# Modulation product of the second block's first layer: from TensorE to GpSimd in a two-block transformer kernel

## The chip, the core and the metric

The kernel runs on one core of a Trainium2 chip. The metric is the device time of one execution in microseconds (us). TensorE (PE) multiplies, VectorE (DVE) and ScalarE (ACT) work elementwise, GpSimd (POOL) works elementwise and issues transfers on a queue of its own, SyncE (SP) only issues transfers; all of them work through their instructions in the order in which the program lists them.

## What is computed

Two blocks in sequence over 256 tokens of 1024 features. The first block has two layers: an attention layer (dilated attention and gated linear attention) and a layer of gated scans. The second block has two layers as well, each a mixer with a feed-forward part, and both of its layers are modulated by a conditioning vector `c`. What matters here are three lines of the second block:

```
c_act = jax.nn.silu(c)
for l in range(DEPTH):
    mod = c_act @ w_ada[l] + b_ada[l]          # [1024] x [1024, 6144]
    sh_m, sc_m, g_m, sh_f, sc_f, g_f = [m[:, None, :] for m in jnp.split(mod, 6, -1)]
    h = rms_norm(x, norm_mix[l]) * (1.0 + sc_m) + sh_m
    ... # mixer; then g_m, sh_f, sc_f, g_f in the feed-forward part
```

`c` doesn't depend on the first block, so `mod` can be computed at any time before its use. For layer 0 of the second block the weights `w_ada[0]` are 6 chunks of 1024 columns, 24 MB in all. Chunks 0 and 1 are needed at the start of the mixer, chunks 2 to 5 behind it.

## The kernel before

**Linear layers.** Every large weight passes through `wtile` (line 210). It loads a block of up to 1 MB over SyncE's queue into a raw tile `wr` (line 220, two buffers), and splits it piece by piece (128 x 1024) into a high part `wh` (ScalarE, line 149) and a rest `wl` (VectorE, line 152). `lin_fm` and `lin_tm` run three matmuls for each pair of tiles: `xTh wh`, `xTh wl`, `xTl wh` (line 172). All matmuls of linear layers accumulate into tiles `pl`.

**The stages.** `layer_ab` runs from 0 to about 237 us: linear layers, two scan groups (class `Scan`, tiles `sc...`, partly on GpSimd), eight attention heads (`attn_a`, line 540), four heads of the linear attention, output layer. Each attention head loads a table `bt` (128 x 2 x 256, 256 KB) over GpSimd's queue (line 543). `layer_c` follows until about 518 us: three groups of linear layers, each with two scan groups on GpSimd, and on GpSimd also `1 - f` of the gates (line 514, tile `cf`). Both layers end with `out_ln` (line 594): its sums over feature tiles (`feat_sum`, tiles `lns`) are added on GpSimd (line 155) before TensorE sums them over the partitions; the layer norm that the next stage starts with waits for these sums. Then come the mixer of the second block's first layer (from about 518 us), its dense feed-forward part (from about 850 us), the second mixer, and the mixture of experts (from about 1406 us to the end).

**The modulation product before.** `ada` (line 699) makes one round of 1024 outputs: eight tiles `adaw` (128 x 1024, 512 KB, two buffers) over SyncE's queue (line 710), and for each of them four matmuls against the activated `c` (tile `adacs`), each in its own 32 rows of one bank `pl`. VectorE adds the bias tile `adao` (loaded by GpSimd, line 720, one buffer), and GpSimd writes the 1024 results to the scratch tensor `modd` (line 715), from which `prep_mod` (line 755, tile `modr`) reads them back as columns. The six rounds are called at: start of `layer_c` (line 458), its third group (line 508), start of the mixer (line 832), behind `solve` (two, line 868), behind the gates (line 886). For the second layer of the second block the product runs on VectorE (`ada_dve`, line 724, called from `wtile` by `self.hook`); that part isn't touched.

**The order.** The program is recorded in program order, and a scheduler orders the instructions of each engine from it before the run. On the chip each engine keeps that order: an instruction that waits holds up all that stand behind it on its engine.

Of the kernel before, what the change touches and what calls it, by code (L numbers as in the profile page):

```python
# [26 lines left out]
F32 = mybir.dt.float32  # L27
# [62 lines left out]
class Net:  # L90
    def __init__(self, ctx, tc, a, out, dump=None):
# [9 lines left out]
        self.hook = self.hold = None  # L101
# [5 lines left out]
        # the 8 banks: linear layers, and two kinds for everything else  # L107
# [34 lines left out]
    def warm(self, ps, cols, n=3, prev=None):  # L142
        """matmuls that keep the tensor engine's clock up while others decide"""
        for _ in range(n):
            i = self.mm(ps[:, :256], cols.to_broadcast([128, 128]), self.c["le1"][:, :256])
            self.behind(i, prev)
# [13 lines left out]
    def behind(self, ins, prev):  # L160
        """order of two instructions of one engine"""
# [16 lines left out]
    def trx(self, out, in_):  # L178
        """transpose into any partition quadrant"""
# [13 lines left out]
    def rsqrt(self, out, in_, scale, eps, pool):  # L193
        """out = (in * scale + eps) ** -0.5, with a step of Newton's method; in is overwritten"""
# [15 lines left out]
    def wtile(self, w, k0, nk, c0, ncol):  # L210
        """rows k0*128.. of w (nk tiles), columns c0..: list of (hi, lo) [128, ncol] per row tile"""
# [13 lines left out]
        for k in range(0, nk, step):  # L225
# [14 lines left out]
            if self.hold and self.hold[0]:  # L240
                self.hold[0] -= 1
                self.behind(ia, self.hold[1])
                self.behind(iv, self.hold[2])
            if self.hook:
# [6 lines left out]
    def mm3(self, out, A, B, start, stop):  # L251
        """out += A^T B with (hi, lo) operands"""
# [5 lines left out]
    def lin_fm(self, X, w, c0, ncols, KT, epi):  # L258
        """feature-major: epi(m0, ps [128, 2, 256]) for output rows m0*128.."""
# [12 lines left out]
    def lin_tm(self, X, w, c0, ncols, KT, epi, step=512):  # L272
        """token-major: epi(c, n, T, ps [128, n]) for output columns c.., token tile T"""
# [15 lines left out]
    def hilo(self):  # L289
        """operand of a layer's first or last product"""  # L290
# [4 lines left out]
    def pair(self, pool, use, dtype=F32):  # L295
        """work tile of two feature tiles; self.tags: where the layer has room for this use"""
# [6 lines left out]
    def feat_sum(self, pool, tag, on, out, first, last):  # L303
        """returns add(v): out [128, 256] = on^T summed over four pairs of feature tiles v [128, 2, 256]"""
# [17 lines left out]
    def load_x(self, pool):  # L322
        """the input, feature-major: residual and operand of the first layer"""
# [17 lines left out]
    def layer_ab(self):  # L341
        nc, tc, a = self.nc, self.tc, self.a
        with ExitStack() as cx:
# [8 lines left out]
            # Toeplitz table of bias and log multiplicity, times 8  # L352
# [14 lines left out]
            # gated linear attention  # L367
# [49 lines left out]
            # dilated attention  # L417
# [18 lines left out]
            # heads of the linear attention, each after its gate  # L436
# [14 lines left out]
    def layer_c(self):  # L451
        nc, tc, a = self.nc, self.tc, self.a
        with ExitStack() as cx:
# [4 lines left out]
            self.ada()  # L458
# [23 lines left out]
            for gr in range(3):  # L482
# [24 lines left out]
                if gr == 2:  # L507
                    self.ada()
# [21 lines left out]
    def load_cols(self, pool, src, n, tag, rtag=None):  # L530
        """rows [n, 128] of DRAM -> columns [128, n]"""
# [39 lines left out]
    def head_norm(self, p2, po, nv, gain, gate, yh, yl, ones, joint, eps=None, raw=None):  # L571
        """po [128, nv, 256]: rms over 128 rows (joint: over all nv*128), times gain, times gate -> hi, lo"""
# [21 lines left out]
    def out_ln(self, pool, Y, w):  # L594
        """z = alpha x + y w, in place of x, and the statistics of its layer norm"""
# [23 lines left out]
    def apply_ln(self, pool, layer, hi=None, lo=None, then=None):  # L619
        """x = layer_norm(z) from the statistics; hi, lo: its operand"""  # L620
# [20 lines left out]
    def square_sum(self, pool, pss, direct=False):  # L641
        """returns add(x): sums of squares over the features, four pairs of feature tiles"""
# [19 lines left out]
    def residual(self, pool, gate, direct=False):  # L662
        """returns epi(m, ps) of x += gate y and the function that ends it with the statistics of the rms norm"""
# [10 lines left out]
    def apply_rms(self, pool, sc, sh, hi, lo):  # L674
        """operand of x * rs * sc + sh"""
# [9 lines left out]
    def ada_init(self):  # L685
# [5 lines left out]
        self.ada_next, self.par, self.hook = 0, {}, None  # L691
# [5 lines left out]
        self.modd = [self.dp.tile([6, 4, 256], F32, name="modd%d" % l) for l in range(2)]  # L697

    def ada(self, n=1):
        """the next n of 6 rounds of silu(c) w_ada + b_ada of the first layer, 1024 values each, into scratch"""  # L700
# [118 lines left out]
    def mixer(self, l):  # L819
        nc, tc, a = self.nc, self.tc, self.a  # L820
        with ExitStack() as cx:
# [45 lines left out]
            if l == 0:  # L867
                self.ada(2)
# [891 lines left out]
```

## Time and profile before

| what | value |
|---|---|
| median of 3 runs | 2498.88 us (2495.86 to 2505.41) |
| span of the profiled execution, first to last instruction | 2500.5 us |
| TensorE, VectorE, ScalarE, GpSimd busy | 95%, 74%, 61%, 17% |
| mean granted TensorE clock | 0.981 of full speed |

The profiled execution has no time of its own beside its span: the span lies within the three runs, 1.6 us above their median. The profile lists instructions by engine and source line, names tiles as `out<-in`, and says for idle time what ended it. Matmuls are pipelined, so that two that follow each other overlap in the table; what one costs is read from the distance of two starts.

### The profile page before, as it was taken

The page shows a single profiled execution, that of the slowest core. Times are in us where ns is not written, and L with a number is a line of the kernel's source. Part 1 is how long each engine was busy: PE and PEld are TensorE (multiplying, and loading weights), DVE is VectorE, ACT ScalarE, POOL GpSimd, SP SyncE. Part 2 cuts the span into 40 slices and gives each one's busy share as a digit, 9 for nine tenths or more (in the row PEclk, how much of TensorE's full clock was granted, in tenths as well). Part 3 has the DMA queues.
Part 4 walks back from the last instruction along what each step waited for, and adds up shares of the span by engine and source line. Part 5 has one row for each costly group of instructions (what it writes and reads, how often), then busy time and mean ns, then how long its engine had stood idle before and what let it go on. Part 6 is the DMA issues. An engine that isn't in the chain of part 4 may idle for free.

```text
span 2500.5 us, 40457 instructions
## 1 busy us (share of the span) xinstructions
PE 2385.5 (95%) x15987; PEld 2016.8 (81%) x15987; DVE 1849.8 (74%) x2516; ACT 1517.0 (61%) x2164; POOL 426.3 (17%) x385
## 2 busy tenths in 40 slices
PE   7998999989999899999999989999999999999998
PEld 7877888868688799998788878787878787877776
DVE  5755777758754676676874578999888889888887
ACT  4654666547444443345754467787777676777765
POOL 2201320221100100001010122222222222222221
PEclk9999999999999899999999899999999999999999
DMA  6454446454443588875322659899999999999994
GB/s 196 150 129 153 154 136 208 144 190 144 123 141 114 174 270 275 279 246 153 102 74 64 236 220 369 317 353 340 368 337 344 330 351 335 339 337 349 329 347 170
DMA packets 335862, 586.90 MB, mean 235 GB/s; under 512 B 29984, under 2 KB 170528, under 8 KB 335664
## 3 DMA queue, kind: packets, MB, share of 16 engines
q1 hardware_dynamic: 321360, 577.28, 67.1%
q0 software_dynamic: 5504, 5.91, 1.3%
q8 instruction: 127, 2.08, 0.4%
q10 hardware_dynamic: 8800, 1.05, 0.3%
q14 instruction: 71, 0.58, 0.1%
HBM read 582.26 MB, written 1.64 MB: 234 GB/s over the span
## 4 chain that ended last, share of the span: by engine, by line
PE 68%; DVE 11%; issue 8%; DMA 5%; ACT 3%; POOL 1%; ACTq 0%; DVEq 0%; POOLq 0%
PE pl L172 43%; PE pn L172 16%; DVE wl L152 7%; PE pm L172 6%; ACT wh L149 2%; DMA wr<-in_w_dense_dram 2%; DMA adaw<-in_w_ada_dram 1%; PE pm L176 1%; PE pn L176 1%; DVE xf L158 1%; DMA wr<-in_w_in_c_dram 1%; DVE es L152 0%; POOL wl L155 0%; DVE ey L152 0%; DMA wr<-in_w_out_dram 0%
## 5 line engine op out<-in xcount | busy, mean ns | idle before, releaser
L152 DVE TENSOR_TENSOR wl<-wr,wh 128x1024 fp32r<-128x1024 f32 (+2 forms) x918 | 1193.0, 1331 | 347.4 <-ACT wh L149 338.1
L149 ACT ACTIVATE wh<-wr 128x1024 fp32r<-128x1024 f32 (+2 forms) x1004 | 1022.2, 1049 | 432.7 <-PE pl L172 229.6
L172 PE MATMUL pl<-wh,eg 128*128 128x512 f32 x1792 | 573.9, 395 | 0.0
L172 PE MATMUL pl<-xTh,wh 128*128 128x256 f32 x1696 | 485.9, 287 | 13.9 <-ACT wh L149 6.9
L172 PE MATMUL pl<-xTh,wl 128*128 128x256 f32 x1696 | 483.1, 286 | 0.3 <-DVE wl L152 0.2
L172 PE MATMUL pl<-xTl,wh 128*128 128x256 f32 x1696 | 482.7, 285 | 0.2 <-DVE xTl L158 0.2
L172 PEld LDWEIGHTS pl<-wh,eg 128*128 128x128 f32 x1792 | 336.8, 188 | 74.0 <-ACT wh L149 0.6
L172 PE MATMUL pl<-wl,eg 128*128 128x512 f32 x896 | 357.0, 398 | 15.8 <-DVE wl L152 11.8
L155 POOL TENSOR_TENSOR wl<-wr,wh 128x1024 fp32r<-128x1024 f32 x86 | 234.1, 2722 | 806.6 <-ACT wh L149 606.5
L172 PEld LDWEIGHTS pl<-xTh,wh 128*128 128x128 f32 x1696 | 324.0, 191 | 23.1 <-ACT wh L149 7.8
L172 PEld LDWEIGHTS pl<-xTl,wh 128*128 128x128 f32 x1696 | 323.7, 191 | 9.7 <-issue 7.7
L172 PEld LDWEIGHTS pl<-xTh,wl 128*128 128x128 f32 x1696 | 322.9, 191 | 9.1 <-issue 7.1
L172 PEld LDWEIGHTS pl<-wl,eg 128*128 128x128 f32 x896 | 168.4, 188 | 65.0 <-DVE wl L152 22.2
L172 PE MATMUL pn<-wl,eah 128*128 128x512 f32 x448 | 177.4, 396 | 4.3 <-DVE wl L152 4.3
L172 PE MATMUL pn<-wh,eal 128*128 128x512 f32 x448 | 174.7, 393 | 3.5 <-DVE eal L152 3.3
L172 PE MATMUL pn<-wh,eah 128*128 128x512 f32 x448 | 149.6, 394 | 3.5 <-ACT eah L149 3.5
L172 PEld LDWEIGHTS pn<-wl,eah 128*128 128x128 f32 x448 | 84.2, 188 | 24.4 <-DVE wl L152 6.6
L172 PEld LDWEIGHTS pn<-wh,eah 128*128 128x128 f32 x448 | 84.1, 188 | 23.7 <-ACT eah L149 5.0
L172 PEld LDWEIGHTS pn<-wh,eal 128*128 128x128 f32 x448 | 83.7, 188 | 21.9 <-DVE eal L152 4.8
L149 ACT ACTIVATE es<-pl 128x512 f32<-128x512 f32 x56 | 33.5, 599 | 93.3 <-PE pl L172 93.1
L172 PE MATMUL pl<-wl,xTh 128*128 128x440 f32 (+2 forms) x208 | 79.2, 381 | 9.1 <-DVE wl L152 9.1
L172 PE MATMUL pl<-wh,xTh 128*128 128x440 f32 (+2 forms) x208 | 74.3, 380 | 8.0 <-ACT xTh L149 5.7
(601 smaller groups left out, 3354.0 us busy)
## 6 DMA issues: line engine op xcount, KB each, us to landing
wr<-in_w_moe_dram SPq DMA_DIRECT2D x336, 1024.0 KB, 7.2
wr<-in_w_dense_dram SPq DMA_DIRECT2D x42, 1024.0 KB, 7.2
wr<-in_w_in_dram SPq DMA_DIRECT2D x32, 1024.0 KB, 5.2
wr<-in_w_in_c_dram SPq DMA_DIRECT2D x30, 1024.0 KB, 5.3
adaw<-in_w_ada_dram SPq DMA_DIRECT2D x48, 512.0 KB, 4.5
adar<-in_w_ada_dram SPq DMA_DIRECT2D x48, 512.0 KB, 5.6
wr<-in_w_in_ab_dram SPq DMA_DIRECT2D x16, 1024.0 KB, 5.3
wr<-in_w_in_dram SPq DMA_DIRECT2D x12, 880.0 KB, 4.7
```

The costliest lines, as they stand in the source:

```text
L149: return self.nc.scalar.activation(out, in_, f, **k)
L152: return self.nc.vector.tensor_tensor(out=out, in0=a, in1=b, op=op)
L155: return self.nc.gpsimd.tensor_tensor(out=out, in0=a, in1=b, op=op)
L158: return self.nc.vector.scalar_tensor_tensor(out=out, in0=a, scalar=s, in1=b, op0=op0, op1=op1)
L172: return self.nc.tensor.matmul(out=out, lhsT=l, rhs=r, start=start, stop=stop, **k)
L176: return self.nc.tensor.transpose(out, in_, self.ident[:k, :k])
```

## The change

`ada` and its six calls go. `ada_init`, in the first layer between the first linear layers and the scans, makes a generator `ada_pool`, and `wtile` takes one step of it for each piece of weights that it splits. 96 steps make the six rounds (8 row tiles, two halves of 512 columns each). A step loads 128 x 512 weights (256 KB) over GpSimd's queue into `adaw` (two buffers, half as wide as before), multiplies them by the column of `adacs` in place on GpSimd, and adds them on GpSimd to `adacc` (128 x 1024, one buffer). The last step of a round lets TensorE sum `adacc` over its partitions in four matmuls against ones, VectorE adds the bias, and GpSimd writes the result to `modd`. `mixer` runs whatever steps are left, before it does anything else. All else of the diff is comments and blank lines.

```diff
@@ wtile, behind the split of one piece
+            if self.hook0:
+                next(self.hook0, None)
@@ layer_c; the same at mixer, three places
-            self.ada()
@@ ada_init
-        self.ada_next, self.par, self.hook = 0, {}, None
+        self.par, self.hook = {}, None
...
+        self.hook0 = self.ada_pool()
@@ ada goes, ada_pool comes
-            ps = self.pl.tile([128, 512], F32, name="pl")
-            o = self.ada_bias(self.aw, 0, r)
-            for k in range(8):
-                raw = self.aw.tile([128, 1024], F32, name="adaw")
-                nc.sync.dma_start(out=raw, in_=w[k * 128:k * 128 + 128, r * 1024:(r + 1) * 1024])
-                for j in range(4):
-                    self.mm(ps[32 * j:32 * j + 32, :256], self.cs[:, k:k + 1].to_broadcast([128, 32]),
-                            raw[:, j * 256:(j + 1) * 256], k == 0, k == 7)
-            self.tt(o, o, ps[:, :256], OP.add)
-            nc.gpsimd.dma_start(out=self.modd[0][r], in_=o[0::32, :])
+        for r in range(6):
+            o = self.ada_bias(self.aw, 0, r)
+            acc = self.aw.tile([128, 1024], F32, name="adacc", bufs=1)
+            for k in range(8):
+                for hf in range(2):
+                    raw = self.aw.tile([128, 512], F32, name="adaw")
+                    c0 = r * 1024 + hf * 512
+                    nc.gpsimd.dma_start(out=raw, in_=w[k * 128:k * 128 + 128, c0:c0 + 512])
+                    v = acc[:, hf * 512:hf * 512 + 512]
+                    if k == 0:
+                        nc.gpsimd.tensor_scalar(v, raw, self.cs[:, 0:1], None, op0=OP.mult)
+                    else:
+                        nc.gpsimd.tensor_scalar(raw, raw, self.cs[:, k:k + 1], None, op0=OP.mult)
+                        nc.gpsimd.tensor_tensor(out=v, in0=v, in1=raw, op=OP.add)
+                    if k == 7 and hf == 1:
+                        ps = self.nbank()[:, :256]
+                        for j in range(4):
+                            self.mm(ps[32 * j:32 * j + 32], self.one.to_broadcast([128, 32]),
+                                    acc[:, j * 256:(j + 1) * 256])
+                        self.tt(o, o, ps, OP.add)
+                        nc.gpsimd.dma_start(out=self.modd[0][r], in_=o[0::32, :])
+                    yield
@@ mixer, first lines
+        for _ in self.hook0 or ():
+            pass
+        self.hook0 = None
```

The order moves at three places. **GpSimd behind the second scan of the first layer**: before, the table transfers `bt` of the heads and the sums `lns` of the output layer follow directly.

```order
L155 TENSOR_TENSOR scF<-scY,scR 128x96
L155 TENSOR_TENSOR scT<-scT,scR 128x32
L155 TENSOR_TENSOR scF<-scY,scT 128x96
L543 DMA bt<-tbd 128x2x256 x6
L155 TENSOR_TENSOR lns_2218<-xf 128x512
```

After, steps of the product stand there in pairs:

```order
L155 TENSOR_TENSOR scF<-scY,scT 128x96
L712 TENSOR_SCALAR adacc<-adaw,adacs 128x512 x2
L532 DMA cw0r<-in_conv_w_dram 48x128
L709 DMA adaw<-in_w_ada_dram 128x512 x2
L714 TENSOR_SCALAR adaw<-adaw,adacs 128x512 x2
L715 TENSOR_TENSOR adacc<-adacc,adaw 128x512 x2
```

The last three rows stand seven times before the next `bt`: two issues, two products that wait for their landing, two sums, and only then the next two issues.

**TensorE at the first head of the attention.** Before, the head (`pn<-ka,qa`) stands among matmuls of a linear layer:

```order
L172 MATMUL pl<-wh,xTh 128x512 x2
L172 MATMUL pn<-ka,qa 128x256 x2
L172 MATMUL pl<-wl,xTh 128x512
L172 MATMUL pl<-wh,xTl 128x512
L172 MATMUL pl<-wl,xTh 128x512
```

After, the sum over the partitions of round 0 (`pn<-adacc,kc`) stands in front of it, and the heads follow each other:

```order
L172 MATMUL pl<-xTh,wl 128x256
L172 MATMUL pn<-adacc,kc 32x256 x2
L172 MATMUL pn<-ka,qa 128x256 x2
L172 MATMUL pn<-bt,cst 128x256 x2
L172 MATMUL pn<-adacc,kc 32x256 x2
L176 MATMUL pm<-ident,as 128x128 x4
L172 MATMUL pn<-apt,va 64x256 x2
L172 MATMUL pn<-ka,qa 128x256 x2
```

Ahead of the first head stood 638 matmuls of linear layers (the scheduler's count, three for each pair of tiles); now there are 864.

**GpSimd at the end of `layer_c`.** Before, the sums `lns` of the output layer follow the last scan:

```order
L155 TENSOR_TENSOR scF<-scY,scR 128x96
L155 TENSOR_TENSOR scF<-scY,scT 128x96
L155 TENSOR_TENSOR lns_5532<-xf 128x512
L155 TENSOR_TENSOR lns_5534<-lnsq 128x512
L155 TENSOR_TENSOR lns_5532<-lns_5532,xf 128x512
```

After, the last pairs, the write of round 5 and the transfer `modr` that reads it back stand between the scan and these sums:

```order
L155 TENSOR_TENSOR scF<-scY,scT 128x96
L715 TENSOR_TENSOR adacc<-adacc,adaw 128x512
L709 DMA adaw<-in_w_ada_dram 128x512 x2
L714 TENSOR_SCALAR adaw<-adaw,adacs 128x512 x2
L715 TENSOR_TENSOR adacc<-adacc,adaw 128x512 x2
...
L722 DMA modd_616<-adao 4x256
L767 DMA modr<-modd_616 32x128
L155 TENSOR_TENSOR lns_5858<-xf 128x512
L155 TENSOR_TENSOR lns_5860<-lnsq 128x512
```

Four pairs stand in the place of the "...", the first of them shown. So all 96 steps stand between the second scan of the first layer and the sums that end the second layer. From the second half of the mixer on, the order of each engine is as before.

## Rows read from the trace of the kernel before

**Rows 1.** Page: span, and the chain of waits by engine.

```profile
span 2500.5 us, 40457 instructions
...
PE 68%; DVE 11%; issue 8%; DMA 5%; ACT 3%; POOL 1%; ACTq 0%; DVEq 0%; POOLq 0%
```

**Rows 2.** Windows: stretch, length, busy us of PE, PEld, DVE, ACT, POOL, clock, DMA share, GB/s.

```profile
97.60:237.00 139.40, 136.65 (x1025) 118.58 (x1026) 75.42 (x132) 67.96 (x119) 12.33 (x13) 1.00 0.46 129
237.00:509.50 272.50, 261.24 (x2469) 231.99 (x2468) 201.32 (x334) 168.09 (x249) 60.86 (x112) 0.97 0.51 166
509.50:538.00 28.50, 18.46 (x119) 12.23 (x117) 12.93 (x25) 10.84 (x20) 10.09 (x17) 0.82 0.66 214
600.00:716.00 116.00, 114.11 (x833) 84.01 (x831) 86.45 (x236) 65.15 (x152) 18.14 (x26) 1.00 0.45 138
```

**Rows 3.** All instructions on tile adaw, the modulation weights; durations in ns.

```profile
L172 PE MATMUL pl<-adaw,adacs x384: 377/379/636, 224.3 to 814.5; 128*32 128x256 f32 x192
L710 SPq DMA_DIRECT2D adaw<-in_w_ada_dram x48: 327/328/1077, 3.3 to 809.8; - x48
...
  DMA adaw<-in_w_ada_dram: 24.7, 13
...
DMA to landing us min/median/max: 3.6/4.5/14.8
```

**Rows 4.** Timeline of TensorE, start of the mixer: start us, us, instruction, idle before.

```profile
528.00 1.08 PE L172 MATMUL pl<-adaw,adacs 128*32 128x256 f32 x8 [3.78 <-DMA adaw<-in_w_ada_dram]
...
532.27 3.87 PE L172 MATMUL pn<-ln,kc 128*128 128x256 f32 x12
538.21 0.47 PE L172 MATMUL pl<-wh,xTh 128*128 128x440 f32 x1 [2.08 <-ACT xTh L149]
```

**Rows 5.** Timeline of TensorE inside the heads of the mixer.

```profile
694.03 0.64 PE L172 MATMUL pl<-adaw,adacs 128*32 128x256 f32 x8
694.59 0.39 PE L172 MATMUL pl<-xTh,wl 128*128 128x256 f32 x1
```

**Rows 6.** Chain of waits, 800 to 850 us: start us, us, what.

```profile
815.68 0.55 POOL modd L715
...
822.11 0.30 PE pm L176
```

**Rows 7.** Groups of GpSimd by line and shape: count | busy us, mean ns | idle before.

```profile
L155 POOL TENSOR_TENSOR mg<-mg,mg 128x512 f32<-128x512 f32 x6 | 9.3, 1544 | 19.4 <-DVE mg L152 19.4
...
L514 POOL TENSOR_SCALAR cf<-cf 128x1024 f32<-128x1024 f32 x6 | 8.5, 1423 | 94.4 <-ACT clf L149 94.4
...
L543 POOL DMA_DIRECT2D bt<-tbd x8 | 5.9, 737 | 76.7 <-PE pn L172 75.1 <-DMA tbd<-tb 1.6
...
L155 POOL TENSOR_TENSOR xf<-xTh,xTl 128x512 f32<-128x512 f32 x4 | 5.0, 1273 | 0.1
L155 POOL TENSOR_TENSOR lns<-xf 128x512 f32<-128x512 f32 x2 | 4.4, 2202 | 81.8 <-DVE xf L158 81.8
```

**Rows 8.** Tile bt, the 256 KB transfers of GpSimd: all eight, issue to landing.

```profile
DMA to landing us min/median/max: 4.7/4.8/8.3
```

**Rows 9.** Tile bt, 28 to 60 us: two such transfers issued together.

```profile
DMA to landing us min/median/max: 6.6/7.5/8.3
```

**Rows 10.** Timeline of GpSimd: end of the second scan, last sum of the second layer.

```profile
97.17 0.39 POOL L155 TENSOR_TENSOR scF<-scY,scT 128x96 f32<-128x96 f32 x1
...
508.26 1.29 POOL L155 TENSOR_TENSOR lns<-lns,lnsq 128x512 f32<-128x512 f32 x1
```

**Rows 11.** Waits of GpSimd: line, waited for: us in total, times, longest.

```profile
POOL adao L720 <- DMA modd<-adao: 34.4, 8, 7.0
```

**Rows 12.** Timeline of TensorE at the first head: spacing of the weight matmuls.

```profile
133.72 1.03 PE L172 MATMUL pn<-bt,cst 128*128 128x256 f32 x4
...
135.06 0.28 PE L172 MATMUL pl<-xTl,wh 128*128 128x256 f32 x1
135.18 0.28 PE L172 MATMUL pl<-xTh,wl 128*128 128x256 f32 x1
```

More of the change, by code (lines that the diff above doesn't have):

```diff
@@ L100, in __init__ @@
         self.wp = E(tc.tile_pool(name="wsplit", bufs=3))
-        self.hook = self.hold = None
+        self.hook = self.hold = self.hook0 = None
         self.wafter, self.moe_on, self.wfirst = None, False, []
@@ L506, in layer_c @@
                 self.lin_fm(X, w, 1536 + c0, 512, 8, epi_f(0))
-                if gr == 2:
-                    self.ada()
                 self.lin_fm(X, w, 3072 + c0, 512, 8, epi_f(1))
@@ L697, in ada_init, with ada_pool @@
         self.modd = [self.dp.tile([6, 4, 256], F32, name="modd%d" % l) for l in range(2)]
-    def ada(self, n=1):
-        nc = self.nc
-        for _ in range(n):
-            r = self.ada_next
-            self.ada_next += 1
-            w = self.a["w_ada_2"][0]
-            ps = self.pl.tile([128, 512], F32, name="pl")
+        self.hook0 = self.ada_pool()
+    def ada_pool(self):
+        nc, w = self.nc, self.a["w_ada_2"][0]
+        for r in range(6):
             o = self.ada_bias(self.aw, 0, r)
+            acc = self.aw.tile([128, 1024], F32, name="adacc", bufs=1)
             for k in range(8):
-                raw = self.aw.tile([128, 1024], F32, name="adaw")
-                nc.sync.dma_start(out=raw, in_=w[k * 128:k * 128 + 128, r * 1024:(r + 1) * 1024])
-                for j in range(4):
-                    self.mm(ps[32 * j:32 * j + 32, :256], self.cs[:, k:k + 1].to_broadcast([128, 32]),
-                            raw[:, j * 256:(j + 1) * 256], k == 0, k == 7)
-            self.tt(o, o, ps[:, :256], OP.add)
-            nc.gpsimd.dma_start(out=self.modd[0][r], in_=o[0::32, :])
+                for hf in range(2):
[16 more added lines that the diff above has]
+                    yield
     def ada_bias(self, pool, l, r):
@@ L831, in mixer @@
             if l == 0:
-                self.ada()
                 pss = self.nbank()[:, :256]
@@ L866, in mixer @@
             oa = solve()
-            if l == 0:
-                self.ada(2)
             mg = [p0.tile([128, 8, 256], F32, name="mg%d" % i, tag=("dq", "mg")[i]) for i in range(2)]
@@ L884, in mixer @@
             gate(0)
-            if l == 0:
-                self.ada()
             self.lin_fm(ob, a["w_ob_2"][l], 0, 1024, 4, branch_b)
```

## Prediction

> **What bounds the kernel now.** First the page: span 2500.5 us, and TensorE holds 68% of the chain of waits that ended last [rows 1]. Then the stretches that the change touches, from the end of the second scan of the first layer to the middle of the mixer [rows 2]: TensorE is busy 98% and 96% of the two long ones, GpSimd 12.33 of 139.4 us and 60.86 of 272.5 us. So up to 509.5 us TensorE is nearly the bound, and GpSimd has some 339 us to spare by its share. The question is whether the steps fit into them one behind the other. From 509.5 to 538 us TensorE is busy 18.46 of 28.5 us at a mean granted clock of 0.82, part of it at the lower of the two levels: the start of the mixer, with a round of the old product in it.
>
> **What goes.** The old product is 384 matmuls on TensorE (192, each in two passes), 48 issues on SyncE, and 24.7 us in which TensorE's two queues sat idle until `adaw` landed [rows 3]; some of it is one wait that both queues show. Eight of the 384 (one weight tile) cost 694.59 - 694.03 = 0.56 us of a full TensorE [rows 5]. Where it counts:
> - Start of the mixer. A group of the old product waits until 528.00 for its tile, and the sums of squares behind it (`pn<-ln`) come at 532.27 and hold up the first weight matmul until 538.21 [rows 4]. Without it these sums can follow ScalarE's squares: I take 6 us off.
> - Rounds 3 to 5 run among other matmuls in the mixer, where TensorE is busy 114 of 116 us [rows 2]: 24 groups x 0.56 = 13.4 us.
> - End of the mixer. The chain goes through the write of round 5 (815.68) and the read of `modr` to a transpose at 822.11 [rows 6]. After the change `modr` is read long before: 6 us off.
> Sum 25 us behind 509.5 us. The rounds before that (0 and 1, 16 groups x 0.56 = 9 us, and a few us of waits) count only if TensorE still bounds that stretch. On SyncE 48 issues of 0.33 us go, which weights no longer wait behind; I cost that at nothing, since after the change the weight transfers would share the engines with the same 24 MB from the other queue.
>
> **What comes.** 96 steps on GpSimd, in pairs, because `adaw` has two buffers and both are given back only by the sums. The order shows one pair: two issues, two products, two sums, then the next issues. Nothing is loaded ahead, so a pair is a round trip. Neither these transfers nor these operations are in the trace; the nearest rows:
> - Issue: 0.74 us (`bt`, also 256 KB) [rows 7]. The second one follows the first, and lands one issue later.
> - Landing: 4.8 us for `bt` alone, 4.7 at least [rows 8]; 6.6 to 8.3 us where two were in flight [rows 9]. The lower bound is 3.6 us, the least of a 512 KB tile of the same weights over SyncE's queue [rows 3]. I take 4.8, the same engine, queue and size.
> - Product, 128 x 512: half of the 1423 ns of 128 x 1024, 0.71 us [rows 7]. Only the second one lies behind the last landing.
> - Sum, 128 x 512: 1.27 us (`xf`) to 2.20 us (`lns`) [rows 7]; I take 1.5, near the 1544 ns of `mg`. Two of them.
> Round trip: 0.74 + 4.8 + 0.71 + 3.0 = 9.25 us, say 9.2. Ends: 0.74 + 3.6 + 0.6 + 2.54 = 7.5, and with a landing of 7.5 us 12.0.
>
> The Trainium skill gives another price (DMA: Bandwidth & Descriptors, section Anatomy of one DMA): a transfer issued from GpSimd takes about 2.0 us plus its bytes at 436 GB/s, that is an estimate of 2.6 us for 256 KB, and a round trip of 7.1 us. Rows 8 do not agree: 4.7 us is the least of eight.
>
> **Where it lies.** GpSimd works in order, and all 96 steps stand between the second scan, which ends at 97.56 us, and the sums `lns` that end `layer_c` (before: 509.55 us [rows 10]). The next stage can't start without those sums. So GpSimd's own time is a floor for that point:
> - start 97.6, products of the first pair (loaded ahead) 1.4;
> - 47 round trips x 9.2 = 432.4;
> - what GpSimd did there before, 12.33 + 60.86 = 73.2 [rows 2];
> - six times between rounds: the write to `modd` and the bias transfer, 1.3 us, and the wait of the second for the first, 34.4 / 8 = 4.3 us [rows 11]: 33.6;
> - minus what overlaps. Some scan pieces, `bt` issues and sums stand between an issue and the product that waits for it, and fill a wait that is there anyway. I take 30 off; the ends are 0 and 73.
> Sum 608 us, 99 us later than 509.55. The floor is also what holds the others up: TensorE's sum of round 0 stands ahead of the first head, so TensorE waits there from about 133.7 + 226 x 0.12 = 160.5 us (the 226 weight matmuls that now stand ahead, at the spacing of [rows 12]) until 97.6 + 1.4 + 7 x 9.2 = 163 us; then the scans of `layer_c`, whose pieces stand between pairs. Linear layers run ahead meanwhile, as far as their tiles allow, so that I add nothing for TensorE's own work behind 608. The half clock in the waits I cost at nothing too: TensorE has time left while it waits for GpSimd, and at the start of the mixer it already was at 0.82.
> Total: 2500.5 + 99 - 25 = 2574.5 us of span. The span is 1.6 us above the median, less than any term is known to: **2575 us**.
>
> **Rivals.**
> - Two in flight land later. If each pair waits as the two `bt` did [rows 9], the round trip is 12.0 us: 47 x 2.8 = 132 us more, 2706 us. For it: the weight blocks use half of the transfer engines in this stretch (share 0.46 and 0.51 [rows 2]). Against: the median of all eight `bt` is 4.8 [rows 8], and most were issued among weight blocks as well.
> - The round trip is short. At 7.5 us, the sum of the lower bounds, the floor falls by 80 us to 528, and the time is 2500.5 + 19 - 25 = 2494: no change that can be measured. It takes a landing below the least of `bt`, and sums beside an idle VectorE. By the rule of the Trainium skill's page (DMA: Bandwidth & Descriptors, section Anatomy of one DMA) it would be about 2475 us on the same working, which hangs on a landing that no row shows.
> - GpSimd isn't the bound: faster. This needs the chain to end before TensorE would, at about 509.55 - 13 = 496 us; from 97.6, with 78 us of other work after overlap, 47 round trips have 496 - 97.6 - 78 = 320 us, so it decides at 6.8 us, or where the order lets far more overlap than I took. Then all of the old product is gain: 25 + 13 = 38 us, 2462 us. But the heads of the attention lose their cover, since 226 weight matmuls moved ahead of them (27 us that used to fill their waits), so that half of the gain may go there. For it: GpSimd's idle share [rows 2]. Against: each round trip is mostly a wait, which idle time elsewhere doesn't shorten.
> - The steps do not stand where the diff puts them. The order rules this out: all 96 are there, and none is left for the mixer.
>
> **Chances.** Forecast (round trips of 8 to 10.5 us) 0.63, its own range 2520 to 2640. Slower landings or more stalls through TensorE and VectorE, which wait in order for each round, 0.16, around 2700. Short round trip 0.12, around 2494. GpSimd not the bound 0.09, 2462 to 2480. A measurement of this kernel tells about 0.5% from no change, 12.5 us. Faster by over that: 0.09 and a little of the short round trip, 0.11. Within: the rest of it, 0.10. Slower: 0.79. The range leaves out the last case and the upper half of the slow one: 2494 to 2680.
>
> **What would show it.** In the trace after: the distance of two pairs of `adaw` issues on GpSimd is the round trip, 9.2 us, most of it idle until `adaw` lands. The sums `lns` of `layer_c` end near 608 us. TensorE is idle in `layer_ab` and `layer_c` for some 100 us, with GpSimd or `adacc` as the releaser, and its clock falls there. The first weight matmul of the mixer comes 6 us sooner behind the last sum than before, and from there to the end it is 25 us shorter in all. The prediction is wrong if the round trip is below 7 us, if the pairs overlap in spite of two buffers, or if GpSimd sits idle for anything but its own transfers in between.

## The result, and the profile after

The changed kernel takes 2656.4 us (median of 4 runs, 2646.4 to 2672.8) against 2499.9 us: 1.064 times as long, 95% interval 1.060 to 1.068. The forecast was 2575 us, with 2680 as the upper end of the range: the way is right, the loss is twice as large as forecast (157 against 75 us). The profiled execution has a span of 2671.0 us, near the top of the runs.

The page shows first that this is no longer a kernel of TensorE alone. Busy time by engine, and the chain of waits by engine and by line (before: TensorE 68%, GpSimd 1% [rows 1]):

```profile
PE 2415.8 (90%) x15651; PEld 2042.0 (76%) x15651; DVE 1909.5 (71%) x2516; ACT 1519.8 (57%) x2164; POOL 774.9 (29%) x661
...
PE 62%; DVE 11%; POOL 11%; DMA 8%; issue 4%; ACT 4%; ACTq 0%; SPq 0%; DVEq 0%; POOLq 0%
```

The windows show where. Columns are start and end, length, busy us of PE, PEld, DVE, ACT and POOL, TensorE's granted clock, DMA share, GB/s. The stretch from the first product to the end of `layer_ab`, and `layer_c`:

```profile
102.00:307.00 205.00, 157.76 (x1054) 125.01 (x1053) 96.35 (x135) 68.28 (x120) 133.39 (x115) 0.83 0.43 128
307.00:695.00 388.00, 285.78 (x2427) 252.94 (x2428) 243.89 (x340) 171.01 (x251) 294.90 (x294) 0.85 0.43 140
```

Before, the two together took 412 us with TensorE busy over 95% at a clock of 1.00 and 0.97 [rows 2]; now they take 592 us, it is busy 75% of them, and the mean clock of 0.84 means that part ran at the lower of its two levels, behind its waits. So the loss lies ahead of one point, the sums `lns` that end `layer_c`: their end moved from 509.6 to 694.4 us (start and length of the last one, from the timeline of GpSimd). The forecast had 608.

```profile
693.10 1.28 POOL L155 TENSOR_TENSOR lns<-lns,lnsq 128x512 f32<-128x512 f32 x1
```

All instructions on `adaw` in the changed kernel, as in [rows 3]; durations in ns (minimum, median, maximum):

```profile
L709 POOL DMA_DIRECT2D adaw<-in_w_ada_dram x96: 536/574/647, 12.0 to 652.0; - x96
L714 POOL TENSOR_SCALAR adaw<-adaw,adacs x84: 1552/1567/3586, 111.0 to 656.2; 128x512 f32<-128x512 f32 x84
L715 POOL TENSOR_TENSOR adacc<-adacc,adaw x84: 1249/1290/2311, 115.5 to 658.9; 128x512 f32<-128x512 f32 x84
L712 POOL TENSOR_SCALAR adacc<-adaw,adacs x12: 1561/1904/3017, 102.0 to 583.4; 128x512 f32<-128x512 f32 x12
...
  DMA adaw<-in_w_ada_dram: 96.2, 41
  PE pn L172: 18.2, 1
...
DMA to landing us min/median/max: 3.0/3.7/7.2
```

The product takes 1.57 us where the forecast had 0.71; the landing 3.7 us (least 3.0) where it had 4.8. The timeline of GpSimd shows one undisturbed pair (start, duration, operation, count, and in brackets the idle time before it):

```profile
232.90 1.09 POOL L709 DMA_DIRECT2D adaw<-in_w_ada_dram  x2
236.01 3.27 POOL L714 TENSOR_SCALAR adaw<-adaw,adacs 128x512 f32<-128x512 f32 x2 [2.02 <-DMA adaw<-in_w_ada_dram]
239.26 2.47 POOL L715 TENSOR_TENSOR adacc<-adacc,adaw 128x512 f32<-128x512 f32 x2
241.68 1.13 POOL L709 DMA_DIRECT2D adaw<-in_w_ada_dram  x2
```

From issue to issue 8.8 us, of which only 2.0 are idle. Last, the longest waits of GpSimd from 102 us to the end of `layer_c`, and of TensorE up to 700 (engine, line, releaser: us in total, times, longest):

```profile
POOL adaw L714 <- DMA adaw<-in_w_ada_dram: 95.3, 40, 5.7
POOL adacc L712 <- PE pn L172: 18.2, 1, 18.2
POOL modr L767 <- PE pm L176: 17.3, 1, 17.3
POOL bt L542 <- PE pn L172: 12.9, 6, 4.3
...
POOL lns L155 <- DVE xf L158: 6.8, 1, 6.8
POOL modd L722 <- DVE adao L152: 6.5, 3, 3.9
POOL cf L513 <- ACT clf L149: 3.1, 1, 3.1
```

```profile
PE pn L172 <- POOL adacc L715: 77.8, 6, 29.5
```

TensorE waits 77.8 us for running sums that GpSimd has not finished; GpSimd waits 65 us for TensorE, VectorE and ScalarE (the rows below the first). Each of the two works in order, and each is held up by the other.

### The profile page after: what moved, and what is told of

Its sections match the earlier page's. It is cut to its first block, busy times and chain, and to the rows that moved or that the text cites. A ratio compares the mean times of both kernels' runs of the same rounds, so it can differ in the third digit from the quotient of the medians.

```text
span 2671.0 us, 40003 instructions
## 1 busy us (share of the span) xinstructions
PE 2415.8 (90%) x15651; PEld 2042.0 (76%) x15651; DVE 1909.5 (71%) x2516; ACT 1519.8 (57%) x2164; POOL 774.9 (29%) x661
## 4 chain that ended last, share of the span: by engine, by line
PE 62%; DVE 11%; POOL 11%; DMA 8%; issue 4%; ACT 4%; ACTq 0%; SPq 0%; DVEq 0%; POOLq 0%
PE pl L172 37%; PE pn L172 17%; DVE wl L152 7%; PE pm L172 6%; DMA adaw<-in_w_ada_dram 4%; POOL adaw L714 4%; POOL adacc L715 3%; ACT wh L149 2%; DMA wr<-in_w_dense_dram 2%; PE pm L176 1%; PE pn L176 1%; POOL adacc L712 1%; DVE xf L158 1%; POOL wl L155 0%; POOL scY L155 0%
## 5 line engine op out<-in xcount | busy, mean ns | idle before, releaser
L152 DVE TENSOR_TENSOR wl<-wr,wh 128x1024 fp32r<-128x1024 f32 (+2 forms) x918 | 1215.1, 1355 | 346.4 <-ACT wh L149 342.8
L714 POOL TENSOR_SCALAR adaw<-adaw,adacs 128x512 f32<-128x512 f32 x84 | 150.8, 1800 | 95.7 <-DMA adaw<-in_w_ada_dram 95.3
L715 POOL TENSOR_TENSOR adacc<-adacc,adaw 128x512 f32<-128x512 f32 x84 | 125.8, 1511 | 0.3
```

The costliest lines, as they stand in the source:

```text
L152: return self.nc.vector.tensor_tensor(out=out, in0=a, in1=b, op=op)
L714: nc.gpsimd.tensor_scalar(raw, raw, self.cs[:, k:k + 1], None, op0=OP.mult)
L715: nc.gpsimd.tensor_tensor(out=v, in0=v, in1=raw, op=OP.add)
```

## Experiments: how much of it is GpSimd, and by what

In all runs below, "end" is the end of the last `lns` of `layer_c` in the profiled execution, and VectorE's time is its busy time from the first product to that end. From this end to the end of the program it is 1963 to 1968 us in e1, e2, f1 and f2, 1977 in the changed kernel, 1957 to 1987 in all runs that leave none of the product to the mixer (e3 apart, see there), and 1991 before. So, to some 15 us, the end of `layer_c` is what the runs are compared by.

| kernel | time, us | ratio to before (95%) | end, us | VectorE, us |
|---|---|---|---|---|
| before | 2500 | 1 | 509.6 | 277 |
| changed | 2656.4 | 1.060 to 1.068 | 694.4 | 340 |
| e1, no product at all | 2473.3 | 0.988 to 0.994 | 501.7 | 278 |
| e2, arithmetic on 4 columns | 2507.7 | 1.001 to 1.007 | 532.9 | 279 |
| f2, product of two operations | 2578.3 | 1.029 to 1.038 | 605.5 | 348 |
| j1, e2 with fillings | 2572.7 | 1.024 to 1.031 | 598.7 | 297 |

**e1, the product left out**:

```
- nc.gpsimd.dma_start(out=raw, in_=w[k * 128:k * 128 + 128, c0:c0 + 512])
- nc.gpsimd.tensor_scalar(raw, raw, self.cs[:, k:k + 1], None, op0=OP.mult)
- nc.gpsimd.tensor_tensor(out=v, in0=v, in1=raw, op=OP.add)
+ if k == 0 and hf == 0:
+     nc.gpsimd.memset(acc, 0.0)
```

> The changed kernel without the 96 transfers, products and sums of the first layer's modulation (the running sum is set to zero once per round, so the modulation is its bias alone); the six sums over partitions on TensorE, the bias transfers and the writes stay. Left out is therefore all that GpSimd does for the product. Theory A (GpSimd's in-order chain of pairs sets when layer_c ends): the last lns falls from 695 to about 500, where TensorE's own work ends, and the time from 2656 to about 2462. Rival B (the order itself costs: heads without the weight matmuls that covered their waits, linear layers behind one another): the chain of GpSimd was only part of it, the heads still wait, lns ends at 530 to 560, time 2490 to 2520.

2473.3 us, end at 501.7, 11 us above theory A's time and at its end: the order of the heads costs nothing that matters, all 183 us of gain come with GpSimd's steps. It is also what this order would give if the product cost nothing, some 27 us less than before.

**e2, transfers without arithmetic.**

```
- nc.gpsimd.tensor_scalar(raw, raw, self.cs[:, k:k + 1], None, op0=OP.mult)
- nc.gpsimd.tensor_tensor(out=v, in0=v, in1=raw, op=OP.add)
+ nc.gpsimd.tensor_scalar(raw[:, :4], raw[:, :4], self.cs[:, k:k + 1], None, op0=OP.mult)
+ nc.gpsimd.tensor_tensor(out=v[:, :4], in0=v[:, :4], in1=raw[:, :4], op=OP.add)
```

> The changed kernel with all its transfers, but each product and each sum over 4 of the 512 columns only, except the first product of each half of a round, which stays whole (so most of the modulation's sum is left out). Landing waits and issues stay, arithmetic goes. Theory A by the measured pieces: a pair falls from 8.7 us (1.1 issues, 2.0 of landing left, 3.1 products, 2.5 sums) to 1.1 + 3.7 + 0.4 = 5.2 us; 48 pairs take 250 us instead of 420, the chain ends near 102 + 250 + 77 = 430, before TensorE is done, so the time falls to that of the kernel without any of it or some 20 us above: 2462 to 2490. Rival C (the landings and the queue are what costs): the pair stays above 7.5 us and the time above 2580.

2507.7 us, 18 above the expectation's upper end, with 85.4 us of waits for landings still there. Transfers, issues, landing waits and the small operations that are left cost 34 us, the arithmetic that was taken out 149. Theory C falls.

**e3, a constant as the scalar; f2, the product as two operations.** Why does a product of 512 columns take longer than the constant one of 1024 from which the forecast had taken its price [rows 7]? First the scalar, `self.cs[:, k:k + 1]` replaced by 0.5:

> The changed kernel with the constant 0.5 in place of the column of the activation as the scalar of each product on GpSimd (the modulation's values are wrong; nothing else differs). It asks why a product of 128x512 took 1.57 us where the constant one of 128x1024 took 1.42. If the per-partition scalar is the cause, the product falls to about 0.71 us; a pair then is 1.1 + 2.0 + 0.7 + 0.9 (product, or the rest of the second landing) + 2.5 = 7.2 us instead of 8.7, 48 x 1.5 = 72 us less on GpSimd's chain, 2580 to 2600 by theory A. If the price belongs to the type, the shape or the place, the product stays at 1.57 and the time at 2656.

The product took 1.49 us: it is not the scalar. (Behind `layer_c` this run is not comparable. It executes some 12,400 more instructions, presumably since other modulations send other tokens to the experts, and 3660 us says nothing of the change.) Then the form; the row of 1024 columns is an instruction of two operations:

```
- nc.gpsimd.tensor_scalar(raw, raw, self.cs[:, k:k + 1], None, op0=OP.mult)
+ nc.gpsimd.tensor_scalar(raw, raw, self.cs[:, k:k + 1], 0.0, op0=OP.mult, op1=OP.add)
```

> The changed kernel with the product written as two operations of one instruction (times the scalar, plus 0.0), as the instruction of 128x1024 that took 1.42 us has two; the values are the same. The run with a constant as the scalar left 1.49 us of the 1.57, so the per-partition scalar is not why the product is dear. If the form with a single operation is, the product falls to about 0.75 us, a pair to 7.2 us and the time by some 72 us to 2575 to 2600. If not, product and time stay as they are (1.57 us, 2656).

```profile
L714 POOL TENSOR_SCALAR adaw<-adaw,adacs x84: 682/700/5060, 105.5 to 558.3; 128x512 f32<-128x512 f32 x84
```

0.70 us instead of 1.57, and 2578.3 us instead of 2656.4: 78 us for adding zero. The forecast's price was right for the form of its row, and the kernel uses the other form.

**e4 and f1, loads ahead.** Written one step ahead (the load of step i + 1 ahead of the product of step i), the transfers should have hidden their landings:

> The changed kernel with each transfer issued one step ahead: the load of step i + 1 stands before the product of step i, in the same two buffers. Nothing is left out. Theory A: 3.4 us of issue, product and sum per step stay (0.57 + 1.57 + 1.25), the landing (3.7 us from its issue) has 2.8 us of arithmetic to hide behind and mostly does, so that the 96 us of waits for landings fall to 20 to 50; 45 to 75 us less, time 2580 to 2610. Rival C (the transfers' own durations bind, the queue serves them no sooner): waits stay near 96 and the time within 15 us of 2656. Rival D (it is not GpSimd's own time but the mutual waits with TensorE and ScalarE): GpSimd is sooner at its steps and waits for the others instead, time 2630 to 2656.

2648.8 us, a miss of theory A: the scheduler still put GpSimd's instructions in pairs (two loads, two products, two sums), and it waited 89.6 us for landings. Program order is not engine order here. With the order pinned:

```
+ nx = load() if todo else None
  i = nc.gpsimd.tensor_scalar(raw, raw, self.cs[:, k:k + 1], None, op0=OP.mult)
+ self.behind(i, nx)
```

> In the run with loads written one step ahead GpSimd's instructions still came in pairs (two loads, two products, two sums), so that it changed nothing and waited 89.6 us for landings. Here the order of one engine is pinned as well: the product of step i is put behind the issue of the load of step i + 1, nothing is left out. Theory A: a step is 0.57 + 1.57 + 1.25 = 3.4 us plus what is left of a landing of 3.2 to 3.7 us behind 2.8 us of arithmetic, 0.4 to 0.9 us: 3.8 to 4.3 instead of 4.4 to 5.4; waits for landings fall from 96 to 40 to 60 us, time 2600 to 2625. If the mutual waits with TensorE take what is saved, the time stays within 15 us of 2656.

2631.1 us, 6 above the expected interval. Waits for landings fell from 96 to 8.1 us and the end came 35 us sooner: the waits for TensorE rose instead (`adacc` 21.5, `bt` 18.6).

**f3 and f4, the steps spread into the mixer** (f4: with the pinned loads of f1):

```
- next(self.hook0, None)
+ self.h0 = getattr(self, "h0", 0) + 1
+ if self.h0 * 96 // 176 != (self.h0 - 1) * 96 // 176:
+     next(self.hook0, None)
```

> The changed kernel with its 96 steps spread evenly over 176 weight blocks, those of the mixer's first half included (rounds 2 to 5 are read only behind the mixer): 70 steps stand ahead of the sums that end layer_c instead of 96, and 26 in the mixer. Nothing is left out. Theory A: 26 steps x 4.4 us = 114 us less on GpSimd's chain ahead of these sums, lns ends near 580, and the mixer has room on GpSimd (26 of 284 us busy): time about 2540, up to 2565 where the steps stand in the way of the mixer's own GpSimd work. If what costs is the product's total on GpSimd wherever it stands, or the order of the heads, the time stays above 2620.

> Both: steps spread over 176 weight blocks and each load pinned ahead of the product of the step before it. Nothing is left out. Theory A: 70 steps x 3.8 to 4.3 us = 266 to 300 us ahead of the sums that end layer_c, with 102 of start and 77 of other work 445 to 480 us plus the mutual waits (65 us with 96 steps, in proportion 47): 492 to 527, just about where TensorE's own work ends (502 without the product). Time 2475 to 2510. If mutual waits don't shrink with the steps, 2530 to 2560.

f3 took 2551.4 us, inside its expectation, but by two errors against each other: the end came at 537.6 and not near 580, and the part behind it grew from 1977 to 2022 us. f4 missed: 2567.7 us, end at 546, not sooner than f3 in spite of the shorter steps. In the mixer GpSimd waited 77.1 us (f3) and 83.4 us (f4) in one piece for TensorE to read the running sum. Fewer us on GpSimd are not the same as a sooner end.

**g1 to g3, every step made cheap.** Half rounds (a running sum of 128x512), three buffers, loads pinned two steps ahead, product of two operations. g3 is g1 spread as f3; g2 is g1 with product and sum on VectorE:

```
- i = nc.gpsimd.tensor_scalar(raw, raw, self.cs[:, k:k + 1], 0.0, op0=OP.mult, op1=OP.add)
- nc.gpsimd.tensor_tensor(out=acc, in0=acc, in1=raw, op=OP.add)
+ i = self.stt(acc, raw, self.cs[:, k:k + 1], acc, OP.mult, OP.add)
```

> The changed kernel with the two-operation product (0.70 us instead of 1.57 in the run before), half rounds one after the other (a running sum of 128x512), which makes room for a third transfer buffer, and each load pinned two steps ahead. Nothing is left out. Theory A: a step is 0.58 issue + 0.70 product + 1.29 sum = 2.6 us, the landing (3.2 us) hides behind two steps; 96 x 2.6 = 247 us, with 100 of start and 77 of other GpSimd work 424, plus mutual waits of 50 to 65 us as far as these come at all: 474 to 490, so that TensorE's own work sets the end of layer_c, at 502 to 515; time 2473 to 2490. If the mutual waits grow into the room (each wait of GpSimd for TensorE is a wait of TensorE for GpSimd later), lns ends at 530 to 560 and the time is 2500 to 2530.

> The transfers stay on GpSimd's queue (three buffers, two steps ahead, half rounds), but the product and the running sum are one instruction of VectorE (1.28 us for 128x1024 in the second layer's modulation, so about 0.65 for 128x512: 84 x 0.65 + 12 x 0.4 = 60 us of VectorE), each pinned behind the rest of the weight block at which it is written. Nothing is left out. Theory A: GpSimd keeps 96 issues x 0.58 = 56 us and waits for buffers rather than landings; VectorE has room (some 330 of 505 us busy ahead of the end of layer_c); lns ends at 505 to 520, time 2475 to 2495. If VectorE's 60 us stand ahead of the rests that TensorE waits for, 2510 to 2540.

> As the run with half rounds, two-operation products and loads two steps ahead, but with the 96 steps spread over 176 weight blocks, into the mixer. Nothing is left out. Spreading had cost 57 us behind layer_c in the two runs that did so (26 steps among the mixer's own GpSimd work), at 4.4 us a step; with 2.6 us it is about 35. Theory A: ahead of layer_c's end GpSimd has 100 + 70 x 2.6 + 77 = 359 us of work, and TensorE sets it (502 to 510); time 2473 + 35 = 2500 to 2515, more than the run that is not spread. If the end of layer_c is still set by GpSimd with 96 steps, spreading gains instead: 2475 to 2490, less than that run.

All three missed theory A's times, and this is where it falls in its bare form: g1 2610.8 us (end 628, waits for landings gone), worse than f2 with its uncovered landings. g2 took 2527.3 us, where the expectation has VectorE's new work standing ahead of the rests (2510 to 2540), and g3 2555.8, above both of its ranges. In g1 the handover of the running sum is the largest wait:

```profile
POOL adacc L722 <- PE pn L172: 58.8, 7, 21.8
POOL modr L780 <- PE pm L176: 25.3, 1, 25.3
POOL bt L542 <- PE pn L172: 24.2, 6, 9.2
```

**h1 to h3, the handover.** TensorE's sums read zeros instead of the running sum (h1: the changed kernel, h2: g1), or there are two running sums in turn (h3: g1).

```
h1  - self.mm(ps[32 * j:32 * j + 32], self.one.to_broadcast([128, 32]), acc[:, j * 256:(j + 1) * 256])
h1  + self.mm(ps[32 * j:32 * j + 32], self.one.to_broadcast([128, 32]), z)
h3  - acc = self.aw.tile([128, 512], F32, name="adacc", bufs=1)
h3  + acc = self.aw.tile([128, 512], F32, name="adacc", bufs=2)
```

> The changed kernel with TensorE's sums over partitions reading a tile of zeros in place of the running sum (so the product's values never enter the modulation, which is its bias alone); transfers, products and sums on GpSimd are all there, with nothing handed over in either direction. Theory A (GpSimd's own time): only the 18.2 us in which GpSimd waited for TensorE to have read the running sum go, lns ends at 660 to 680, time 2625 to 2645. Theory E (the handover couples the two in-order engines: each wait of one is a wait of the other later): the other waits of GpSimd for TensorE, ScalarE and VectorE (some 47 us) go too, in part or whole, lns ends at 625 to 655, time 2585 to 2620.

> The run with half rounds, cheap products and loads two steps ahead (2611), with TensorE's sums reading zeros in place of the running sum, so that nothing is handed over (the modulation is its bias alone). Theory A + E: GpSimd's own work is 100 + 96 x 2.6 + 77 = 424 us, its waits no longer couple; lns ends where TensorE's own work does, 505 to 530, time 2475 to 2500. If the handover is not what costs, GpSimd's other waits stay (some 90 us) and the time is 2570 to 2600.

> The run with half rounds, cheap products and loads two steps ahead, with two running sums in turn instead of one (room for it by letting two small tiles share a place). Nothing is left out. Theory E: the 58.8 us in which GpSimd waited for the one running sum to be read fall to below 15, and a part of the waits behind them (bt 24, modr 25, lnbr 16) goes too: lns ends at 545 to 580 instead of 628, time 2520 to 2560. If these waits only move to the next thing that GpSimd shares with TensorE, lns stays above 600 and the time above 2590.

h1 took 2525.7 us, below both theories, and is not clean: with nothing waiting for them the scheduler moved 24 of the 96 loads behind the end of `layer_c`. h2 keeps all steps ahead: 2556.1 us, end at 573.8 instead of 628, so that the handover was worth 54 us there; but it missed 2475 to 2500 by over 50, and lies between its two ranges. h3 missed too, between its two ranges: 2578.5 us, end at 617, 11 us sooner than g1; the wait for the running sum went, but those for `modr` (25.3 to 34.5 us) and `modd` (6.1 to 28.8) grew and the one for `bt` stayed (24.8).

**i1, i2 and j1, what arithmetic does beside its own time.** In h2 GpSimd's last step ends at 533 us, nothing is handed over, and yet the end is 72 us later than in e1. VectorE was busy for 379 us instead of 278 with the same work. Here is one of its operations with two inputs in SBUF, in the trace of before, of the changed kernel and of h2 (count, then busy us and mean ns of one):

```profile
L152 DVE TENSOR_TENSOR scK<-scK,scF 128x256 f32<-128x256 f32 x42 | 15.7, 420 | 0.2 <-PE pm L172 0.2
```

```profile
L152 DVE TENSOR_TENSOR scK<-scK,scF 128x256 f32<-128x256 f32 x42 | 22.2, 547 | 0.0
```

```profile
L152 DVE TENSOR_TENSOR scK<-scK,scF 128x256 f32<-128x256 f32 x42 | 31.9, 768 | 0.0
```

So product and sum were replaced by fillings with zeros, which read nothing and were meant to take as long (i1 from h2, i2 from the changed kernel, three for a product and two for a sum there):

```
- nc.gpsimd.tensor_scalar(raw, raw, self.cs[:, k:k + 1], None, op0=OP.mult)
- nc.gpsimd.tensor_tensor(out=v, in0=v, in1=raw, op=OP.add)
+ nc.gpsimd.memset(raw, 0.0)
...
+ nc.gpsimd.memset(v, 0.0)
...
```

> The run without handover (half rounds, loads two steps ahead, 2556), with each product replaced by one filling of the tile with zeros (0.54 us in the trace of before, for 0.70) and each sum by two of the running sum (1.07 for 1.29): GpSimd is busy for nearly as long but reads no operand (the modulation is its bias alone, product and sum are left out). Theory F (contention: GpSimd's operations that read tiles hold up VectorE's with two operands): VectorE's busy time up to the last lns falls from 379 to about 280 us, lns ends at 505 to 525 instead of 573, time 2473 to 2495. Theory A (GpSimd's own time in order): 96 x 0.4 = 38 us less on GpSimd at most, lns at 540 to 570, time 2520 to 2555.

> The changed kernel with each product replaced by three fillings with zeros of 128x512 (1.6 us for 1.57) and each sum by two (1.07 for 1.29); transfers, order of the steps, the one running sum and its handover to TensorE stay (the modulation is its bias alone, product and sum are left out). It asks what of the changed kernel's loss is contention with VectorE. Theory A: GpSimd's chain is shorter by 96 x 0.2 = 19 us and by the 29 to 38 us by which its operations were stretched beside VectorE: lns ends at 640 to 660 instead of 695, time 2600 to 2625. Theory F (VectorE's slowdown is most of it): VectorE falls from 340 to 280 us and the engines behind it catch up, lns at 580 to 630, time 2540 to 2595.

i1 took 2493.2 us (end 518.7), inside theory F's ranges; i2 2506.4 us (end 536.2), beyond them. But a filling needs no scalar, so these chains began between 11 and 20 us instead of 102; and GpSimd was busy on the steps for 182 us (i1; h2: 286) and 277 us (i2; changed kernel: 351). So three effects are mixed. e3 began nearly as early as i2 and reads its operands: its end was at 637.9, 102 us behind i2's, but its steps keep GpSimd busy for 332 us, 55 more than i2's. j1 keeps start and dependences and comes nearer in the durations (edit: e2, plus two fillings of 508 columns behind each product and each sum, in pinned order):

> The run with products and sums over 4 of 512 columns (2508), in which each product is followed by two fillings of the rest of its tile and each sum by two of the rest of the running sum, in this order: 0.30 + 2 x 0.54 = 1.38 us for the product (1.57 in the changed kernel), 0.20 + 2 x 0.54 = 1.28 for the sum (1.29). GpSimd's chain starts, waits and hands over as in the changed kernel and is busy for nearly as long, but reads almost nothing (most of the modulation's sum is left out). Theory A (own time in order): 96 x 0.19 = 18 us and 38 us of stretched operations less, lns at 630 to 645 instead of 695, time 2590 to 2610. Theory F (reads beside VectorE): VectorE's busy time from 102 us to the last lns falls from 340 to 280 to 290 us, and the waits between the engines with it: lns at 560 to 600, time 2530 to 2565.

2572.7 us, end at 598.7: the end at the upper edge of theory F's range (560 to 600; A had 630 to 645), the time between the two (F 2530 to 2565, A 2590 to 2610). In j1, two operations of VectorE:

```profile
L169 DVE TENSOR_SCALAR cf<-cf,om,l 128x256 f32<-128x256 f32 x24 | 16.9, 744 | 1.2 <-ACT cf L149 1.2
...
L152 DVE TENSOR_TENSOR scK<-scK,scF 128x256 f32<-128x256 f32 x42 | 16.4, 416 | 0.0
```

The two-input one is back at its time of before, although GpSimd is as busy (75% of the stretch, 72% in the changed kernel); the other (408 ns before, 548 in the changed kernel) is still slowed. The Trainium skill has this rule (SBUF — State Buffer, section Who interferes with whom): VectorE with two inputs in SBUF contends with a GpSimd instruction that reads SBUF, not with one that only writes it, and copies and scalar operations of VectorE, where they run in one of its two-port modes, contend with GpSimd too. These rows agree, and the forecast did not weigh it, beside a VectorE that was busy two thirds of this stretch (277 of 412 us).

By the ends of `layer_c`, then: transfers, issues and small operations 31 us (e1 to e2), fillings in the place of the arithmetic another 66 (e2 to j1), product and sum in the place of the fillings another 96 (j1 to the changed kernel). The last 96 are not the price of the reads alone, since j1 differs in two more things. In its order more of the landings is hidden: waits of 48.5 us instead of 96.2. And its steps are shorter: each filling starts before the one ahead of it has ended (start, then length):

```profile
233.96 0.51 POOL L729 MEMSET adacc<- 128x508 f32 x1
234.42 0.51 POOL L726 MEMSET adaw<- 128x508 f32 x1
234.91 0.19 POOL L727 TENSOR_TENSOR adacc<-adacc,adaw 128x4 f32<-128x4 f32 x1
```

From start to start, in medians over the trace, product and sum with their fillings take 2.27 us in j1, product and sum of the changed kernel 2.80; GpSimd was busy on the steps for 308 us instead of 351. These two differences make 91 of the 96 us, and GpSimd's other waits are not fewer in j1 (75 us against 68). So j1 does not decide between the theories: the changed kernel's end less 48 us of landing waits and 43 us of busy time is 604 us, by GpSimd's own time in order alone. Shown is that products and sums on GpSimd slow VectorE down (340 us against 297 in j1); what that costs at the end of `layer_c`, beside the handover, is not shown.

## Why the forecast was right in its way and wrong in its size

The sum, term by term, from the end of the second scan to the end of the last `lns`. Steps are GpSimd's busy time on the product and its waits for landings; all other waits are what is left:

| term, us | forecast | changed kernel | f2, product at 0.70 us |
|---|---|---|---|
| first product | 97.6 | 102.0 | 99.4 |
| 96 steps | 1.4 + 432.4 = 433.8 | 351.1 + 96.2 = 447.3 | 269.6 + 74.1 = 343.7 |
| other GpSimd work | 73.2 | 77.2 | 73.4 |
| all other waits | 33.6 - 30 = 3.6 | 67.9 | 89.0 |
| end of `layer_c` | 608 | 694.4 | 605.5 |

- **GpSimd's chain as the bound, slower than before**: right, as a floor. The steps stand one behind the other between the two points that the forecast named, and e1 takes all of the loss away. The rivals of a short round trip and of GpSimd not being the bound are out.
- **The step that failed is "minus what overlaps ... I take 30 off" together with "I add nothing for TensorE's own work".** GpSimd's own time is a floor, but the chain does not run at its floor: all other waits came to 67.9 us and not 3.6, 64 of the 86 us that are missing at this point. They are waits for TensorE to read the one running sum (18.2), to take the last `modr` (17.3) and to be done with `bt` (12.9), and for VectorE and ScalarE (16.4). The forecast saw that TensorE waits for GpSimd; it did not follow the loop back to GpSimd. Shorter steps do not take these waits away: they were 89.0 us in f2, 171 in g1, and 106 in h2, where nothing is handed over. The half clock, which the forecast cost at nothing, is in this loop too: TensorE was busy for 443 us of the stretch instead of 398, with about as many matmuls (3478 against 3493) at a mean clock of 0.84 instead of 0.98. How much of that reaches the end is not shown.
- **The round trip was right in its sum by two errors.** 9.2 us forecast, 447.3 / 48 = 9.3 measured. The product was priced at 0.71 us from an instruction of another form and is 1.57, and both products of a pair lie behind the landing's rest, not one; the landing was priced at 4.8 us from `bt` and is 3.7. "The same engine, queue and size" did not make it the same landing.
- **f2 hits the forecast (2578 against 2575) and does not confirm it**: its steps are 90 us shorter than forecast, its other waits 85 us longer. It does show that the product's form is worth 78 us.
- **VectorE and GpSimd side by side** had no term at all: 63 us more of VectorE's busy time, and product and sum with medians of 1567 and 1290 ns, but maxima of 3586 and 2311. What part of the loss this is stays open (j1).
- **25 us back behind `layer_c`**: right in the runs e1, e2, f1 and f2 (1963 to 1968 against 1991 us, 23 to 28); 14 in the profiled execution of the changed kernel, and between 4 and 34 over all runs without steps in the mixer (e3 apart). The start of the mixer gave 4 of the 6 us: from the last matmul of `layer_c` to the first weight matmul of the mixer 19.0 us, before 23.
- **The rule for the landing** (the Trainium skill, DMA: Bandwidth & Descriptors, section Anatomy of one DMA; an estimate of 2.6 us by its formula): the least of 96 was 3.0 us and the median 3.7, so that it was as far below as the 4.8 us taken were above.
- **The rival "two in flight land later"** came nearer to the result (2706) by a mechanism that did not happen: the landings were shorter than assumed, not longer.

No version here that computes everything beats the kernel before. The nearest is g2 (2527.3 us, 1.006 to 1.014), and in this order, with the product for nothing (e1), 27 us would be left to gain.

## What to carry to other kernels

Idle share does not say that an engine can take work: ask how many round trips stand in a row on it, and who waits for each, in both directions, because two in-order engines that hand one buffer back and forth pay each other's waits. Take a duration from a row of the same operation in the same form; a row of twice the size with another number of operations was wrong by a factor of two. Before moving arithmetic to GpSimd, look at what VectorE does meanwhile, and cost its two-input operations as slower.

## What the runs showed of the hardware that was not expected

- A GpSimd `TENSOR_SCALAR` of 128x512 in fp32 takes 1.57 us with one operation (1.49 with a constant) and 0.70 us with two, the second of which adds zero. Why is not shown.
- A VectorE `TENSOR_TENSOR` of 128x256 rose from 420 to 768 ns on average beside GpSimd's products and sums (h2), and stayed at 416 beside fillings that kept GpSimd as busy as in the changed kernel (j1).
- Transfers of 256 KB from GpSimd's queue landed 3.0 us after their issue at the least and 3.7 in the median; `bt` of the same size had 4.8 [rows 8].
